# An mLSTM recurrence in one kernel: values projected with tokens on the partitions, decays of four heads joined, the loop turned by one chunk

## The chip, the cores and the metric

The kernel runs on one core of one Trainium2 chip. The metric is the device time of one execution in microseconds (us). Before the change the median of 3 runs is 1986.46 us (1985.74 to 1988.04).

## The reference, cut to what matters

One layer of a decoder: a half-step SwiGLU, a mixer, a second SwiGLU and a gated embedding, all in float32 on 1024 tokens of width 1024. The change lies in the mixer's mLSTM group (4 heads; queries and keys of 64, values of 128 numbers each):

```python
z = u @ w_in[i]
m_qk, m_v, m_o, m_if, f_q, f_k, f_v, f_f = jnp.split(z, split_idx, axis=-1)
m_qk = jax.nn.silu(causal_depthwise_conv(m_qk, conv_qk[i]))
...
# mlstm_chunkwise, per chunk: what was carried in (C), what the chunk's own tokens add (P)
D = jnp.where(causal, b[..., :, None] - b[..., None, :] + log_i[..., None, :], -jnp.inf)
P = jnp.exp(D - m_t[..., None]) * jnp.einsum("bhcld,bhcsd->bhcls", q, k)
num = (w_inter[..., None] * jnp.einsum("bhcld,bhcde->bhcle", q, C_prev)
       + jnp.einsum("bhcls,bhcse->bhcle", P, v))
C_new = decay[..., None, None] * C + jnp.einsum("bhl,bhld,bhle->bhde", w, k_c, v_c)
...
y_m = head_rmsnorm(h_m, mlstm_out_norm[i]) * jax.nn.sigmoid(m_o)
```

## The kernel before, in words

Large products are done three times in a rounded float32 (fp32r): `mm3` (L118) multiplies high by high, high by low and low by high part. A projection of 128 columns of `w_in` is a job of `proj_stream`: for each half of the tokens, 8 steps over the depth, each step 3 matmuls of 128x512, all 24 into one PSUM bank, which a "sink" then empties. The weights were split into parts earlier and lie in DRAM (`wD`); `ready_cols` loads a job's four tiles (`whi`, `wlo`, 256 KB each), one job ahead.

`mlstm` runs four stages. First the gates and the query and key columns are projected (`qk_sink`), with the gates' arithmetic woven between. Half of the gates' product was made earlier and goes through DRAM: `begun` is stored to `eD` and loaded as `G` (L791, L819). Then the values are projected: the result has value columns on the partitions, so `v_sink` copies it (`vt`) and `v_turn` transposes it, four 128x128 pieces at a time (L966), into `v1`, where tokens are on the partitions. Then the recurrence, `main`, goes through 8 chunks of 128 tokens; the projection of the output gates (`fill`, 64 steps) is woven between its pieces by estimated costs. Last, FoX attention begins with its own projections into `acc`.

A chunk of `main` has these pieces on TensorE:

- decays: `d` gets the mask (L1009, 128x512) and for each of the 4 heads one small product that spreads a row of 36 partitions (L1012, `sel` as weights); ScalarE makes `E` from it.
- scores: `st`, 4 products of 64 rows (L1023), and two transposes of the keys (L1031) for `kw`.
- outputs: for each pair of heads the carried state times the queries (L1039, 128x258) and the scores times the values (L1041, twice 128x129), into `num`.
- state: for each pair `dl` (L1044, 128x258), which VectorE adds into the state `C`.

These are plain float32, and each float32 product stands in the profile as two matmul records. After chunks 3 and 7 `back` transposes the normalised rows `ysb` (L1088), multiplies by the output gate and stores them. A scheduler of the framework moves instructions of neighbouring pieces past each other within limits, so the built order differs a little from the written one.

Of the kernel before, what the change touches and what calls it, by code (L numbers as in the profile page):

```python
# [9 lines left out]
F32 = mybir.dt.float32  # L10
# [6 lines left out]
P = 128  # L17
# [666 lines left out]
def proj_stream(N, xt, jobs, bank=None, begun=None):  # L684
# [5 lines left out]
    nxt = begun or get(0)  # L690
# [38 lines left out]
def run_all(gen):  # L729
    for _ in gen:  # L730
        pass
# [9 lines left out]
class Mix:  # L741
# [14 lines left out]
    def consts(self, pool):  # L756
# [9 lines left out]
        nc.vector.tensor_copy(out=self.mask_r, in_=m)  # L766

# [36 lines left out]
    def gates(self, xt, keep, gp, bank):  # L804
# [101 lines left out]
        s32 = t("X", shape=(36, 6, P))  # L906
        nc.gpsimd.memset(s32, 0.0)
        for row in (0, 32):
            nc.gpsimd.affine_select(out=s32[row:row + 4, 0:4, :], in_=s32[row:row + 4, 0:4, :], pattern=[[-1, 4], [0, P]],
                                    compare_op=ALU.not_equal, fill=1.0, base=0, channel_multiplier=1)  # L910
            nc.gpsimd.affine_select(out=s32[row:row + 4, 4:6, :].rearrange("p a (b c) -> p a b c", b=2),
                                    in_=s32[row:row + 4, 4:6, :].rearrange("p a (b c) -> p a b c", b=2),
                                    pattern=[[-2, 2], [-1, 2], [0, 64]],
                                    compare_op=ALU.not_equal, fill=1.0, base=0, channel_multiplier=1)
        self.sel = keep.tile([36, 6, P], F32R, tag="sel", name="sel")
# [3 lines left out]
    def mlstm(self, xt, keep):  # L919
        nc, N = self.nc, self.N  # L920
        with ExitStack() as ctx:
            pool = lambda name, **kw: ctx.enter_context(self.tc.tile_pool(reuse_waits="tile", name=name, **kw))
            mk, mps = pool("mk", bufs=1), pool("mps", bufs=1, space=PSUM)
            mt = None
            qk = mk.tile([P, 4, S], F32, tag="qk", name="qk")
            v1 = mk.tile([P, NCH, 4, 129], F32, tag="v1", name="v1")
            G1 = mk.tile([P, 4, S], F32, tag="G1", name="G1")
            qw = mk.tile([P, 2, S], F32, tag="qw", name="qw")
            dec = mk.tile([P, 2, NCH], F32, tag="dec", name="dec")
            nc.gpsimd.memset(v1[:, :, :, 128:129], 1.0)  # L930
            zin = {}

            def qk_sink(ct):
                def sink(half, acc):
# [4 lines left out]
                    zh = zt[:, 3 + half * 512:515 + half * 512]  # L939
                    if acc is None:  # L940
# [14 lines left out]
            def v_sink(hd):  # L955
                def sink(half, acc):
                    vt = mt.tile([P, 512], F32, tag="vt", name="vt")
                    nc.scalar.copy(out=vt, in_=acc)
                    turned.append((vt, half, hd))
                return sink  # L960

            def v_turn():
                vt, half, hd = turned.pop(0)
                pt = N.tr()
                for j in range(4):
                    nc.tensor.transpose(pt[:, j, :], vt[:, j * P:(j + 1) * P], N.ident)  # L966
                nc.vector.tensor_copy(out=v1[:, 4 * half:4 * half + 4, hd, 0:128], in_=pt)

# [8 lines left out]
            bank = lambda: mps.tile([P, 512], F32, tag="num", name="pj", bufs=2)  # L977
# [5 lines left out]
            turned = []  # L983
# [3 lines left out]
            v_turn()  # L987

            def main():

                for pr in range(2):
                    wb = mk.tile([P, S], F32, tag="zin", name="wb", bufs=2)
                    for half in range(2):
                        d = mps.tile([P, 512], F32, tag="D", name="wd")
                        nc.tensor.matmul(d, self.sel[:, 4 + pr, :], self.RW[:, half * 512:half * 512 + 512],
                                         start=True, stop=True)
                        nc.scalar.activation(out=wb[:, half * 512:half * 512 + 512], in_=d, func=AF.Exp)
                        yield 0.22
# [3 lines left out]
                C = [mk.tile([P, 258], F32, tag=f"C{pr}", name=f"C{pr}") for pr in range(2)]  # L1002
                for pr in range(2):
                    nc.gpsimd.memset(C[pr], 0.0)
                ysb, todo = {}, []
                for c in range(NCH):
                    ts = slice(c * P, c * P + P)
                    d = mps.tile([P, 4, P], F32, tag="D", name="d")
                    nc.tensor.matmul(d.rearrange("p a b -> p (a b)"), self.mask_r, self.ident_r.unsqueeze(1).to_broadcast([P, 4, P]),  # L1009
                                     start=True, stop=False)  # L1010
                    for hd in range(4):
                        nc.tensor.matmul(d[:, hd, :], self.sel[:, hd, :], self.R[:, ts], start=False, stop=hd == 3)  # L1012
                    E = mt.tile([P, 4, P], F32, tag="E", name="E")
# [3 lines left out]
                    yield 0.9  # L1017
                    PT = mt.tile([P, 2, 2, P], F32, tag="PT", name="PT")
                    for a in range(2):
                        o = 64 * a  # L1020
                        st = mps.tile([P, 2, P], F32, tag="ST", name="st", bufs=2)
                        for pr in range(2):
                            nc.tensor.matmul(st[:, pr, :], qk[o:o + 64, 2 + pr, ts], qk[o:o + 64, pr, ts], start=True, stop=True)  # L1023
                        nc.vector.scalar_tensor_tensor(out=PT[:, :, a, :], in0=st, scalar=0.125, in1=E[:, a:4:2, :],
                                                       op0=ALU.mult, op1=ALU.mult)
                    yield 0.9

                    if c < NCH - 1:
# [3 lines left out]
                        kw = mt.tile([P, 4, 64], F32, tag="kw", name="kw", bufs=1)  # L1032
                        nc.vector.tensor_tensor(out=kw, in0=kt[:, 0:2, :].rearrange("p a (b c) -> p (a b) c", b=2),
                                                in1=self.tok[:, c, 1, :].unsqueeze(2).to_broadcast([P, 4, 64]), op=ALU.mult)
                        yield 0.3
                    for pr in range(2):
# [5 lines left out]
                        if c < NCH - 1:  # L1042
                            dl = mps.tile([P, 258], F32, tag="D", name="dl")
                            nc.tensor.matmul(dl, kw[:, 2 * pr:2 * pr + 2, :].rearrange("p a c -> p (a c)"),  # L1044
                                             v1[:, c, 2 * pr:2 * pr + 2, :].rearrange("p a c -> p (a c)"), start=True, stop=True)
                            for a in range(2):
                                Cd = C[pr][64 * a:64 * a + 64, 129 * a:129 * a + 129]
                                dd = dl[64 * a:64 * a + 64, 129 * a:129 * a + 129]
                                if c == 0:
                                    nc.vector.tensor_copy(out=Cd, in_=dd)  # L1050
                                else:
                                    nc.vector.scalar_tensor_tensor(out=Cd, in0=Cd, scalar=dec[64 * a:64 * a + 64, pr, c:c + 1],
                                                                   in1=dd, op0=ALU.mult, op1=ALU.add)
                        yield 1.4

                        dn = N.sp.tile([P, 2], F32, tag="dn2", name="dn2")
                        nc.vector.tensor_copy(out=dn, in_=num[:, :, 128])
                        nc.vector.scalar_tensor_tensor(out=dn, in0=dn, scalar=-1.0, in1=dn, op0=ALU.mult, op1=ALU.max)
                        nc.vector.tensor_tensor(out=dn, in0=dn, in1=self.tok[:, c, 2, 2 * pr:2 * pr + 2], op=ALU.max)
                        nc.vector.scalar_tensor_tensor(out=dn, in0=dn, scalar=EPS, in1=dn, op0=ALU.mult, op1=ALU.mult)  # L1060
                        sq = mt.tile([P, 2, P], F32, tag="sq", name="sq", bufs=1)
                        nc.scalar.activation(out=sq, in_=num[:, :, 0:128], func=AF.Square)
                        ss = N.sp.tile([P, 2], F32, tag="ss2", name="ss2")
                        nc.vector.tensor_reduce(out=ss, in_=sq, axis=AX.X, op=ALU.add)
                        nc.vector.scalar_tensor_tensor(out=dn, in0=ss, scalar=1.0 / 128, in1=dn, op0=ALU.mult, op1=ALU.add)
                        r = N.rsqrt(dn)
                        if c % 4 == 0:
                            ysb[c // 4, pr] = (mk, mt)[c // 4].tile([P, 2, 4, P], F32, tag=("zin", "ysb")[c // 4], name="ysb", bufs=2)
                        nc.vector.tensor_tensor(out=ysb[c // 4, pr][:, :, c % 4, :], in0=num[:, :, 0:128],
                                                in1=r.unsqueeze(2).to_broadcast([P, 2, P]), op=ALU.mult)  # L1070
                    if c % 4 == 3:
                        todo += [(c // 4, pr) for pr in range(2)]
                    for item in [x for x in todo if x[1] in opened]:
                        todo.remove(item)
                        yield from back(ysb[item], *item)
                while todo:
                    if todo[0][1] in opened:
                        yield from back(ysb[todo[0]], *todo.pop(0))
                    else:
                        yield None  # L1080
# [553 lines left out]
```

## Time and profile before

| what | value |
|---|---|
| median of 3 runs | 1986.46 us |
| the profiled execution: its time, its span | 1986.16 us, 1984.3 us |
| TensorE (PE) busy | 1949.5 us, 98% of the span |
| VectorE (DVE), ScalarE (ACT), GpSimd (POOL) busy | 67%, 44%, 5% |
| granted TensorE clock, mean | 0.999 of full speed |

The profile shows for each engine when each instruction ran. PE is matmul, PEld weight load, SP the engine that issues DMAs. Matmuls overlap: a record of 0.39 us may be followed by the next one 0.23 us later, so what a matmul costs is read from start to start, not from its duration.

### The profile page before, as it was taken

The numbers are of one execution on the slowest core, as the hardware profiler recorded it, in microseconds if no ns is written. First come the engines' busy times: TensorE is split into PE (matmuls) and PEld (weight loads), VectorE is DVE, ScalarE is ACT, GpSimd is POOL, SyncE is SP. The second block draws the span as 40 slices with busy tenths as digits, with TensorE's granted clock in tenths as the row PEclk, the third lists the DMA queues.
The fourth block names the chain that finished last, engine by engine and source line by source line (L and its number), as shares of the span: only waits on it lengthen the run. The fifth ranks groups of instructions, "written<-read, shape, count | busy, mean of one in ns | idle before, by whom it ended". The sixth has DMA issues, their size and how long they took to land. (4 is left out here: it accounts for less than half of the span.)

```text
span 1984.3 us, 25653 instructions
## 1 busy us (share of the span) xinstructions
PE 1949.5 (98%) x9155; PEld 1607.3 (81%) x9155; DVE 1325.5 (67%) x2295; ACT 876.5 (44%) x1686; POOL 97.2 (5%) x118
## 2 busy tenths in 40 slices
PE   7999999999999999999999999999999999999998
PEld 6788888888888888778888888788888888888786
DVE  7877766776877762554665766965665565877766
ACT  6544444444445332334555543533333333445444
POOL 1100000000000110110000001200000000000011
PEclk9999999999999999999999999999999999999999
DMA  7877877778533343133222846632333337633322
GB/s 276 261 245 233 270 243 237 253 234 297 187 96 112 103 148 101 52 127 109 75 79 81 299 149 229 224 110 80 111 113 95 100 118 271 210 107 108 122 75 85
DMA packets 251920, 318.70 MB, mean 161 GB/s; under 512 B 16440, under 2 KB 158288, under 8 KB 251024
## 3 DMA queue, kind: packets, MB, share of 16 engines
q1 hardware_dynamic: 251792, 317.06, 48.5%
q8 instruction: 72, 1.18, 0.3%
q14 instruction: 56, 0.46, 0.1%
HBM read 205.73 MB, written 107.09 MB: 158 GB/s over the span
## 5 line engine op out<-in xcount | busy, mean ns | idle before, releaser
L118 PE MATMUL pp<-xhi,whi 128*128 128x512 f32 x704 | 275.1, 391 | 2.1 <-DVE xn L238 1.5
L118 PE MATMUL pp<-xhi,wlo 128*128 128x512 f32 x704 | 274.8, 390 | 0.0
L118 PE MATMUL pp<-xlo,whi 128*128 128x512 f32 x704 | 274.0, 389 | 0.0
L118 PE MATMUL dn<-xhi,whi 128*128 128x512 f32 x528 | 205.6, 389 | 0.1
L118 PE MATMUL dn<-xlo,whi 128*128 128x512 f32 x528 | 205.4, 389 | 0.0
L118 PE MATMUL dn<-xhi,wlo 128*128 128x512 f32 x528 | 205.1, 389 | 0.0
L125 ACT CAST whi<-raw 128x512 fp32r<-128x512 f32 x152 | 94.0, 622 | 172.8 <-PE pp L118 118.9
L125 ACT CAST whi<-ar 128x512 fp32r<-128x512 f32 x132 | 82.3, 623 | 195.5 <-PE dn L118 180.4
L118 PEld LDWEIGHTS pp<-xhi,whi 128*128 128x128 f32 x704 | 132.1, 188 | 30.7 <-DVE xn L238 1.3
L118 PEld LDWEIGHTS pp<-xlo,whi 128*128 128x128 f32 x704 | 132.7, 188 | 27.9 <-DVE xlo L126 0.3
L118 PEld LDWEIGHTS pp<-xhi,wlo 128*128 128x128 f32 x704 | 132.2, 188 | 27.8
L126 DVE TENSOR_TENSOR wlo<-ar,whi 128x512 fp32r<-128x512 f32 x132 | 90.8, 688 | 77.9 <-ACT whi L125 77.7
L126 DVE TENSOR_TENSOR wlo<-raw,whi 128x512 fp32r<-128x512 f32 x152 | 103.8, 685 | 43.2 <-ACT whi L125 27.4
L118 PEld LDWEIGHTS dn<-xhi,whi 128*128 128x128 f32 x528 | 99.1, 188 | 21.0 <-DVE t L311 0.5
L118 PEld LDWEIGHTS dn<-xlo,whi 128*128 128x128 f32 x528 | 99.1, 188 | 20.7
L118 PEld LDWEIGHTS dn<-xhi,wlo 128*128 128x128 f32 x528 | 99.1, 188 | 20.5
L125 ACT CAST vhi<-S 128x512 fp32r<-128x512 f32 x88 | 54.7, 621 | 104.7 <-PE pp L118 73.0
L125 ACT CAST whi<-S 128x512 fp32r<-128x512 f32 x88 | 54.6, 620 | 98.4 <-PE pp L118 52.8
L130 POOL TENSOR_TENSOR r<-v,mhalf 128x1 f32<-128x1 f32 (+1 forms) x56 | 43.7, 781 | 1094.8 <-DVE v L139 725.6
L126 DVE TENSOR_TENSOR wlo<-S,whi 128x512 fp32r<-128x512 f32 x88 | 62.0, 704 | 51.8 <-ACT whi L125 37.6
L118 PE MATMUL pj<-xhi,whi 128*128 128x512 f32 x200 | 84.6, 423 | 0.9 <-ACT zin L943 0.8
L126 DVE TENSOR_TENSOR tl<-tr,th 128x512 fp32r<-128x512 f32 (+2 forms) x112 | 55.4, 497 | 42.3 <-ACT th L125 40.4
(341 smaller groups left out, 4546.2 us busy)
## 6 DMA issues: line engine op xcount, KB each, us to landing
ar<-hidD SPq DMA_DIRECT2D x60, 512.0 KB, 3.4
hidD<-t SPq DMA_DIRECT2D x110, 256.0 KB, 3.2
raw<-in_ffn_w_gate_dram SPq DMA_DIRECT2D x46, 512.0 KB, 3.9
raw<-in_ffn_w_up_dram SPq DMA_DIRECT2D x46, 512.0 KB, 4.9
wD<-whi SPq DMA_DIRECT2D x64, 256.0 KB, 2.2
wD<-wlo SPq DMA_DIRECT2D x64, 256.0 KB, 2.3
raw<-in_w_in_dram SPq DMA_DIRECT2D x24, 512.0 KB, 4.4
whi<-wD SPq DMA_DIRECT2D x48, 256.0 KB, 2.7
```

The source lines that it names most:

```text
L118: mm = lambda *a, **kw: self.nc.tensor.matmul(*a, skip_group_check=more, **kw)
L125: self.nc.scalar.copy(out=hi, in_=src)
L126: return self.nc.vector.tensor_tensor(out=lo, in0=src, in1=hi.bitcast(F32), op=ALU.subtract)
L130: self.nc.gpsimd.tensor_tensor(out=r, in0=v, in1=self.mhalf[:, :v.shape[-1]], op=ALU.pow)
```

## The change

The values are projected the other way round: the tokens' tile `xt` is the stationary operand and the weights stream past it, so tokens come out on the partitions and `v_turn` is gone. All value weights must then be there at once: two tiles `wv` of 2 MB each, filled by 8 loads of 512 KB, two at each of the first four calls of `qk_sink`. The four spreading products of a chunk become one 128x512 product of a matrix of ones with `Rb`, the rows of `R` times a 0/1 pattern `own`, made by VectorE. The loop is written out: a chunk's outputs and state and the next chunk's scores stand together, its decays come two chunks ahead, and `pump(n)` places n steps of the output gate projection (3 matmuls each). Norms of the two pairs are joined, and `num` is copied to `ysb` first.

```diff
-            for n, _ in enumerate(proj_stream(N, xt, [(C_MV + hd * P, v_sink(hd), None) for hd in range(4)], bank)):
-                if n % KT == 3 and turned:
-                    v_turn()
+            loads = [(i, part) for i in range(4) for part in range(2)]
+            def load_wv():
+                for i, part in loads[:2]:
+                    nc.sync.dma_start(out=wv[part][:, i].bitcast(F32), in_=N.wD[:, 4 + i, part, :].rearrange("p (k n) -> p k n", k=KT))
+                del loads[:2]
...
+            for c in range(NCH):
+                acc = bank()
+                ts = slice(c % 4 * P, c % 4 * P + P)
+                for k in range(KT):
+                    xh, xl = xt[c // 4][k // 4]
+                    N.mm3(acc, xh[:, k % 4, ts], xl[:, k % 4, ts], wv[0][:, :, k, :], wv[1][:, :, k, :], k == 0, k == KT - 1)
+                nc.scalar.copy(out=v1[:, c, :, 0:128], in_=acc.rearrange("p (a b) -> p a b", a=4))
...
-                    for hd in range(4):
-                        nc.tensor.matmul(d[:, hd, :], self.sel[:, hd, :], self.R[:, ts], start=False, stop=hd == 3)
+                    nc.vector.tensor_tensor(out=rb[0:36], in0=self.R[:, chunk(c)].bitcast(F32).unsqueeze(1).to_broadcast([36, 4, P]),
+                                            in1=self.own.unsqueeze(2).to_broadcast([36, 4, P]), op=ALU.mult)
+                    nc.tensor.matmul(flat, self.ones_r, rb.rearrange("p a b -> p (a b)"), start=False, stop=True)
...
+                for c in range(NCH):
+                    nums = outputs(c)
+                    state(c)
+                    if c + 1 < NCH:
+                        scores(c + 1)
+                    norm(c, nums)
...
+                    pump(2 if c == 0 else 4)
+                    if c + 2 < NCH:
+                        decays(c + 2)
+                    pump(2 if c == 0 else 4)
```

What the built programs do with it is shown at three places. First PE where the values are projected. Before, the rows are fill after fill, and each bank's transposes follow after a few steps of the next one (`vt` is the copied bank):

```order
L118 MATMUL pj<-xhi,whi 128x512
L118 MATMUL pj<-xlo,whi 128x512
L118 MATMUL pj<-xhi,wlo 128x512
L966 MATMUL tr<-ident,vt 128x128 x4
L118 MATMUL pj<-xhi,whi 128x512
```

After the change, with buffer numbers (`wv_6277` is the high, `wv_6281` the low part; the first row is the last of the key projection):

```order
L118 MATMUL pj_6580<-xhi_5784,wlo_6492 128x512
L118 MATMUL pj_6664<-wv_6277,xhi_5778 128x512
L118 MATMUL pj_6664<-wv_6281,xhi_5778 128x512
L118 MATMUL pj_6664<-wv_6277,xlo_5779 128x512
L118 MATMUL pj_6664<-wv_6277,xhi_5778 128x512
```

Nothing but such rows stands there now, 192 of them, where 192 projections and 32 transposes stood.

Second, PE in a chunk of the loop. Before, the decays, one step of `fill`, and the scores:

```order
L1009 MATMUL d<-ident_r,mask_r 128x512
L1012 MATMUL d<-R,sel 128x128 x4
L118 MATMUL pj<-xhi,whi 128x512
L118 MATMUL pj<-xlo,whi 128x512
L118 MATMUL pj<-xhi,wlo 128x512
L1023 MATMUL st<-qk 128x128 x4
L118 MATMUL pj<-xhi,whi 128x512
```

After, the decays stand between two runs of 12 projections:

```order
L118 MATMUL pj<-xlo,whi 128x512
L118 MATMUL pj<-xhi,wlo 128x512
L1024 MATMUL d<-ident_r,mask_r 128x512
L1025 MATMUL d<-Rb,ones_r 128x512
L118 MATMUL pj<-xhi,whi 128x512
```

and all the rest of the chunk in one block (here with the transposes of the first `back`):

```order
L1060 MATMUL num<-C_6876,qw 128x258
L1062 MATMUL num<-v_6662,PT 128x129 x2
L1060 MATMUL num<-C_6877,qw 128x258
L1062 MATMUL num<-v_6662,PT 128x129 x2
L1073 MATMUL dl<-v_6662,kw 128x258 x2
L1037 MATMUL st<-qk 128x128 x4
L1041 MATMUL tr<-ident,qk 128x128 x2
L1142 MATMUL tr<-ident,ysb 128x128 x4
```

The four float32 pieces that `fill` used to part are now next to each other, and 24 projections follow instead of 21. From the first FoX projections that follow the last `ysb` transposes, PE's order is the same in both programs.

Third, SP's queue while the gates are projected. Before:

```order
L791 DMA eD<-begun 128x512
L813 DMA gbias<-in_b_fox_f_dram 8x1
L819 DMA G<-eD 128x512
L1380 DMA hr<-hD 128x1024
L791 DMA eD<-begun 128x512
L1380 DMA hr<-hD 128x1024
L89 DMA whi<-wD 128x512
```

After, with five of the eight loads of `wv` ahead of `G` (one more stands above this piece):

```order
L941 DMA wv<-wD 128x1024 x2
L795 DMA eD<-begun 128x512
L941 DMA wv<-wD 128x1024 x2
L823 DMA G<-eD 128x512
L795 DMA eD<-begun 128x512
L941 DMA wv<-wD 128x1024
L89 DMA whi<-wD 128x512
L953 DMA zin<-eD 128x512
L89 DMA wlo<-wD 128x512
```

The loads of `wv` have moved in front of the store to `eD` and the load of `G`; the loads of `hr`, which belong to a later stage, come after them.

## Rows read from the trace of the kernel before

**Rows 1.** Two stretches: busy us (records) by engine; clock, DMA share, GB/s.

```profile
699.00:710.00 11.00, 11.00 (x52) 9.03 (x51) 0.96 (x2) 6.31 (x8) 0.00 (x0) 1.00 0.81 272
...
815.00:825.00 10.00, 10.00 (x55) 7.71 (x53) 5.54 (x23) 2.38 (x7) 1.39 (x2) 1.00 0.16 53
```

**Rows 2.** Waits of PE from 745 to 889 us.

```profile
PE num L1041 <- DVE PT L1024: 0.4, 1, 0.4
PE d L1009 <- DVE C L1052: 0.4, 1, 0.4
```

**Rows 3.** Timeline of PE, a run of projections: start, duration, instruction.

```profile
730.02 0.39 PE L118 MATMUL pj<-xhi,whi 128*128 128x512 f32 x1
...
737.50 0.39 PE L118 MATMUL pj<-xhi,whi 128*128 128x512 f32 x1
```

**Rows 4.** Timeline of PE, the transposes of one value bank.

```profile
777.10 0.60 PE L966 MATMUL tr<-ident,vt 128*128 128x128 f32 x4
...
778.48 0.39 PE L118 MATMUL pj<-xlo,whi 128*128 128x512 f32 x1
```

**Rows 5.** Timeline of PE, one chunk of the loop.

```profile
815.09 0.47 PE L1009 MATMUL d<-ident_r,mask_r 128*128 128x512 f32 x1
815.49 0.66 PE L1012 MATMUL d<-R,sel 36*128 36x128 f32 x4
...
816.64 0.40 PE L118 MATMUL pj<-xhi,wlo 128*128 128x512 f32 x1
...
817.62 0.33 PE L1031 MATMUL tr<-ident,qk 128*128 128x128 f32 x1
817.86 0.50 PE L118 MATMUL pj<-xhi,whi 128*128 128x512 f32 x1
818.19 0.40 PE L118 MATMUL pj<-xlo,whi 128*128 128x512 f32 x1
...
819.46 0.60 PE L1039 MATMUL num<-C,qw 128*128 128x258 f32 x2
...
820.34 0.60 PE L1044 MATMUL dl<-v,kw 128*128 128x258 f32 x2
...
821.01 0.39 PE L118 MATMUL pj<-xlo,whi 128*128 128x512 f32 x1
...
824.96 0.46 PE L1009 MATMUL d<-ident_r,mask_r 128*128 128x512 f32 x1
```

**Rows 6.** Timeline of PE, a 128-column mask product in the FoX stage.

```profile
921.92 0.22 PE L1202 MATMUL acc<-mask_r,ident_r 128*128 128x128 f32 x1
921.98 0.45 PE L1203 MATMUL acc<-k,q 68*128 68x512 f32 x1
```

**Rows 7.** Groups of ACT, 793 to 892 us: busy us, mean ns, idle before.

```profile
L1015 ACT ACTIVATE E<-d,tok 128x128 f32<-128x128 f32 x32 | 9.1, 368 | 12.7 <-PE d L1012 12.7
...
L997 ACT ACTIVATE wb<-wd 128x512 f32<-128x512 f32 x4 | 2.4, 598 | 2.5 <-PE wd L995 2.5
L997 ACT ACT_TABLE_LOAD x1 | 1.3, 1283 | 0.0
```

**Rows 8.** Groups of DVE from 793 to 892 us.

```profile
L1024 DVE SCALAR_TENSOR_TENSOR PT<-st,E 128x256 f32<-128x256 f32 x16 | 6.1, 419 | 7.6 <-PE st L1023 5.0 <-ACT E L1015 2.6
...
L126 DVE TENSOR_TENSOR ylo<-yg,yhi 128x512 fp32r<-128x512 f32 x8 | 5.5, 688 | 1.6 <-DMA yD<-ylo 0.7 <-ACT yhi L125 0.7
```

**Rows 9.** Timeline of SP's issues while the gates are projected.

```profile
694.15 0.35 SPq L791 DMA_DIRECT2D eD<-begun  x1
...
696.21 0.35 SPq L819 DMA_DIRECT2D G<-eD  x1
```

**Rows 10.** ACT there; in brackets its idle time and what ended it.

```profile
699.48 0.72 ACT L820 ACTIVATE G<-G,gbias 128x512 f32<-128x512 f32 x1 [0.93 <-DMA G<-eD]
...
705.29 0.69 ACT L820 ACTIVATE G<-pj,gbias 128x512 f32<-128x512 f32 x1 [4.14 <-PE pj L118]
```

**Rows 11.** Timeline of PE, later in the gates' stage.

```profile
722.40 0.50 PE L118 MATMUL pj<-xhi,whi 128*128 128x512 f32 x1 [0.83 <-ACT zin L943]
```

More of the change, by code (lines that the diff above doesn't have):

```diff
@@ L681, in weave, with proj_stream @@
         assert cost is not None
-def proj_stream(N, xt, jobs, bank=None, begun=None):
+def proj_stream(N, xt, jobs, bank=None, begun=None, first=None):
     def get(j):
@@ L953, in qk_sink @@
                 return sink
[L955 to L967, printed above, removed]
             def o_sink(hd):
@@ L1016, in main, with scores @@
                                              bias=self.tok[:, c, 0, hd:hd + 1])
[L1017 to L1026, printed above, removed]
+                def scores(c):
+                    ts = chunk(c)
+                    sts = [mps.tile([P, 512], F32, tag="ST", name="st", bufs=2)[:, 0:256].rearrange("p (a b) -> p a b", a=2) for _ in range(2)]
+                    for pr in range(2):
+                        for a in range(2):
+                            o = slice(64 * a, 64 * a + 64)
+                            nc.tensor.matmul(sts[a][:, pr, :], qk[o, 2 + pr, ts], qk[o, pr, ts], start=True, stop=True)
                     if c < NCH - 1:
@@ L1041, in main @@
                             nc.tensor.matmul(num[:, a, :], PT[:, pr, a, :], v1[:, c, 2 * pr + a, :], start=c == 0, stop=c == 0 or a == 1)
[L1042 to L1066, printed above, removed]
+                        nums.append(num)
@@ new lines, in outputs, with state @@
+                    return nums
+                def state(c):
+                    if c == NCH - 1:
+                        return
+                    kw = kws.pop(c)
+                    dls = []
+                    for pr in range(2):
+                        dl = mps.tile([P, 258], F32, tag="D", name="dl") if pr else N.tr("dl").rearrange("p a b -> p (a b)")[:, 0:258]
+                        nc.tensor.matmul(dl, kw[:, 2 * pr:2 * pr + 2, :].rearrange("p a c -> p (a c)"),
+                                         v1[:, c, 2 * pr:2 * pr + 2, :].rearrange("p a c -> p (a c)"), start=True, stop=True)
+                        dls.append(dl)
+                    for pr, dl in enumerate(dls):
+                        for a in range(2):
+                            Cd = C[pr][64 * a:64 * a + 64, 129 * a:129 * a + 129]
+                            dd = dl[64 * a:64 * a + 64, 129 * a:129 * a + 129]
+                            if c == 0:
+                                nc.vector.tensor_copy(out=Cd, in_=dd)
+                            else:
+                                nc.vector.scalar_tensor_tensor(out=Cd, in0=Cd, scalar=dec[64 * a:64 * a + 64, pr, c:c + 1],
+                                                               in1=dd, op0=ALU.mult, op1=ALU.add)
@@ new lines, in main @@
+                decays(0)
+                pump(0)
+                scores(0)
+                decays(1)
+                pump(2)
+                for c in range(NCH):
+                    if c == 7:
+                        self.first = N.ready_cols(TILES.index(C_FV))
+                    nums = outputs(c)
[3 more added lines that the diff above has]
+                    norm(c, nums)
+                    for item in [x for x in todo if x[1] in opened][:1]:
+                        todo.remove(item)
+                        back(ysb[item], *item)
+                    pump(2 if c == 0 else 4)
+                    if c + 2 < NCH:
+                        decays(c + 2)
+                    pump(2 if c == 0 else 4)
@@ L1071, in main @@
                     if c % 4 == 3:
                         todo += [(c // 4, pr) for pr in range(2)]
[L1073 to L1080, printed above, removed]
+                pump(64)
@@ L1082, in back @@
+                for item in todo:
+                    back(ysb[item], *item)
             def back(y, half, pr):
@@ L1093, in back, with pump @@
                     self.put_y(mt, hd, half, yg)
-                    yield 0.5
             opened = []
-            fill = proj_stream(N, xt, [(C_MO + hd * P, o_sink(hd), None) for hd in range(4)])
-            weave(main(), fill, 0.9)
+            fill = proj_stream(N, xt, [(C_MO + hd * P, o_sink(hd), None) for hd in range(4)], first=first)
+            def pump(n):
+                for _ in range(n):
+                    next(fill, None)
+            main()
     def put_y(self, pool, k, half, src, gain=None, bufs=2, tags=("yhi", "ylo")):
@@ L1341, in attention @@
                     yield tick()
-            run_all(proj_stream(N, xt, jobs(0), bank))
+            run_all(proj_stream(N, xt, jobs(0), bank, first=self.first))
             self.wf = []
```

96 lines of the change are left out of this document (68 added, 28 removed).

## The prediction

> **What bounds the kernel now.** I first read the busy times by stretch, to see which engine the mLSTM stage waits for. In the loop PE is busy 10.00 of 10 us at clock 1.00 (the 2.4 GHz level), VectorE 5.54 and ScalarE 2.38 [rows 1]. Then the waits: from 745 us, where the value projection starts, to 889 us, where the last transposes of the stage are done, PE waits twice, 0.4 us each [rows 2]. So nothing is late there. The time goes into the instructions on PE themselves and into what it costs to pass from one kind to the next, and only a change in that list can win much. Third, the timeline of PE read from start to start. In an undisturbed run 33 projections start within 737.50 - 730.02 = 7.48 us, 0.227 us each [rows 3]. Against this price I measure everything else.
>
> **The value projection.** It keeps its 192 matmuls of 128x512. Which operand is stationary and which streams is exchanged; weight loads are as many as before. What goes is the transposes. One bank: from 777.10 to 778.48 us there are four transposes and four projections; 1.38 - 4 x 0.227 = 0.47 us [rows 4]. Eight banks: **3.8 us less**. The VectorE copies behind them vanish too, but nobody waited for them.
>
> The new streaming operand lies in four pieces of 128 columns. No row before has such an operand. From below it costs nothing more. From above, a piece may cost what a separate 128-column product does, 0.06 us [rows 6], so 0.24 in place of 0.227: 192 x 0.013 = 2.5 us. I take nothing, since the pieces stay one instruction.
>
> **The decays.** Before: from 815.09 to 816.64 us stand the mask, four spreading products and two projections, 1.55 - 0.45 = 1.10 us [rows 5]. The mask's own step is 0.40 us, so the four products and the return cost 0.70. After: mask and one 128x512 product with all 128 partitions, between projections of the same kind. The new product should cost one step, 0.227; the mask between 0.227 and its present 0.40. Together 0.45 to 0.63; I take 0.50, nearer to the low end because the mask's next weights no longer have 36 rows. Saved 0.60 a chunk, eight chunks: **4.8 us less** (3.8 to 5.2). VectorE gets one product of 36x512 a chunk, priced by the 128x512 subtraction at 0.69 us [rows 8]; it has over 4 us of idle time in each 10 [rows 1].
>
> A rule of the Trainium skill speaks against this term. TensorE: Matmul & The Clock Gate, section "Back-to-back issue gap", has a matmul cost its columns at 2.4 GHz plus about 2.5 ns; four of 128 columns would then cost as much as one of 512. The 0.70 us above against 0.227 does not agree with it; by the rule alone this term would be near nothing.
>
> **The rest of the chunk.** The chunk takes 824.96 - 815.09 = 9.87 us and holds 21 projections (4.77); less the decays, 4.00 us remain [rows 5]. Its pieces: a state product and two value products 820.34 - 819.46 = 0.88, twice; `dl` up to the second projection after it 821.01 - 820.34 - 0.227 = 0.44, twice; scores from 816.64 to 817.62 less one projection, 0.75; first transpose 0.24; second about 0.11; the return to projections 818.19 - 817.86 - 0.227 = 0.10 [rows 5]. Set side by side, the block needs 1.76 + 0.88 + 0.65 (no change of kind ahead of the scores) + 0.35 + 0.10 = 3.74. Saved 0.26, eight chunks: **2.1 us less**. The two old waits of 0.4 us go as well, since 24 projections now stand behind each block: **0.8 us less**. A floor for this part is 0.8, a ceiling about 3.2 if the scores' pairs overlap better.
>
> **New waits.** In a steady chunk I see none. The longest chain is `dl`, four updates of `C` on VectorE, next outputs; between lie 24 projections, 5.4 us. `d` has one buffer and is shared with `dl`: `E` takes 4 x 0.37 = 1.5 us [rows 7], behind the decays, and 12 projections (2.7 us) hide it. If that cover were gone it would cost PE 1.5 us a chunk.
>
> At the loop's start there is less cover. One table load 1.28, four exponentials 2.4, `Rb` at most 0.69, `E` 1.5, `PT` 0.84 make a chain of 6.7 us [rows 7, 8], without the wide product for `qw` and the hand-overs. PE has 21 projections (4.8 us), two decays (1.0), scores and transposes (1.0), one `dl` (0.44) and the four products for `wd` at 0.23 or more, 8 us or so in all, and then for the first chunk only few projections. I take **1.0 us more** for start and end of the loop. Nothing is the lower bound; 3 us the upper one, two unhidden `E`.
>
> **The loads.** `wv` is 8 x 512 KB in place of 16 x 256 KB, but now all in the gates' stage. Five stand ahead of `G` in SP's queue. `eD` was stored at 694.15, `G` issued at 696.21 and used at 699.48 after ScalarE had waited 0.93 us for it [rows 9, 10]. In the busiest stretch nearby the DMA engines moved 272 GB/s at share 0.81 [rows 1]; 512 KB take 1.9 us at that speed. One load was issued long before; four can be ahead: 4 x 1.9 = 7.7 us, so `G` would be there at about 706 instead of 699.48. ScalarE's next job was only due at 705.29 [rows 10], which hides most of it. What comes late after that is the gates' chain, on which PE already waits 0.83 us at 722.40 [rows 11]; this wait grows by the delay. **0.3 us more**, bounds 0 and 3. SP's queue holds the weights of the next key columns behind `wv` as well, but these are a whole job (10.9 us) ahead. The late loads of `hr` serve a stage hundreds of us away. The values' own weights are needed at 745 us and stand in SP's queue between the weights of the first key jobs.
>
> **Sum.** 3.8 + 4.8 + 2.1 + 0.8 - 1.0 - 0.3 = 10.2 us. The profiled execution took 1986.16 us, 0.3 under the median of the runs shown. 1986.16 - 10.2 + 0.3 gives 1976.3; I say 1976.2.
>
> **Rivals.**
>
> *The dense block makes its own waits.* Where `fill` parted the pieces, VectorE had time between them. If each chunk loses 0.6 us to a hand-over (a `C` update queued behind a norm that waits for GpSimd, say), 8 x 0.6 = 4.8, and the time is 1981. For it: before, PE waited only where work was bunched [rows 2]. Against it: 5.4 us of projections per chunk and a VectorE that is half idle [rows 1]. 0.12.
>
> *A matmul costs its columns and nothing else.* Then joining four products and grouping pieces saves nothing, and only the transposes go, 8 x 4 x 0.11 = 3.5 us at the 0.11 of the second key transpose; less 1.3 of new waits, the time is about 1984. For it: the 128-column mask product of the FoX stage costs 0.06 us, a quarter of 0.227 [rows 6]. Against it: the 0.70 of four such products with 36 rows [rows 5]. 0.05. This is the rule of the skill named above.
>
> *The change doesn't do what it says: the pieces stream slower.* At 0.24 the time is 1978.7; from 0.282 a matmul on (192 x 0.055 = 10.5) it is no faster. 0.05, nearly all of it at the mild end.
>
> *Slower: the loads starve the gates' stage.* Place: `G` and the first weights of the key columns behind `wv`. If each of the three loads of key weights, at 1.9 us for every `wv` ahead, came after the matmul that needs it and `G` 7 us late, PE would stand still for up to 12 us, and the time would be 1988. It decides from 10 us of such waits on. Against it: a share of 0.81 in the busiest stretch leaves room [rows 1], and the `hr` loads no longer stand there. 0.06. The Trainium skill, DMA: Bandwidth & Descriptors, section "Queues, rings and completion order", says that an issuing engine owns one ring on each DMA engine and that descriptors are consumed in ring order; by that, `G` does queue behind `wv`. The load of `G` landing 3.3 us after its issue is too little to show it here.
>
> **How the numbers follow.** Forecast 0.72, rivals as above. The forecast's terms alone span about 1973 (all at their best, no waits: 13 us) to 1979. To 1982.2 the range takes in the dense block's waits, the slow pieces, or start and `G` at their upper bounds together. What is left out is the columns rule and the slower case, and some tails. No change is within 0.2% of the median, 4 us, about what a measurement tells. Faster takes the forecast, most of the first rival and the mild pieces: 0.87; same 0.08; slower 0.05.
>
> **What would show it.** Right: no L966 on PE and 192 value projections 0.227 us apart; mask and L1025 together about 0.5 us; from the end of the key projection to the last `ysb` transposes some 11 us less than before; PE's waits in the loop under 2 us; the wait at 722 us about as long as now. Wrong: value projections over 0.25 us apart; waits of PE on `num` or `d` in every chunk; ScalarE waiting several us for `G` and PE behind it.

## The result: 12.4 us faster, and where they came from

The changed kernel takes 1973.99 us (median of 4 runs, 1971.42 to 1975.25), the kernel before 1986.39 us (4 runs, 1985.74 to 1988.04). The ratio is 0.9936, 95% interval 0.9924 to 0.9948. The profiled execution took 1973.56 us, its span is 1971.8 us.

To find the place I use two marks that both kernels have: ScalarE's last copy of keys and queries, and TensorE's first FoX product. Here they are in the timeline of the kernel before (start, duration, instruction, and in brackets ScalarE's idle time ahead of it):

```profile
745.41 0.58 ACT L943 COPY zin<-pj 128x512 f32<-128x512 f32 x1 [4.81 <-PE pj L118]
...
881.82 0.48 PE L118 MATMUL acc<-xhi,whi 128*128 128x512 f32 x1
```

and in that of the changed kernel, with two turns of `y` that stand a little later:

```profile
745.04 0.59 ACT L955 COPY zin<-pj 128x512 f32<-128x512 f32 x1 [4.81 <-PE pj L118]
...
868.71 0.48 PE L118 MATMUL acc<-xhi,whi 128*128 128x512 f32 x1
...
875.00 0.66 PE L1142 MATMUL tr<-ident,ysb 128*128 128x128 f32 x4
875.41 0.48 PE L118 MATMUL acc<-xhi,wlo 128*128 128x512 f32 x1
```

The stage went from 136.41 to 123.67 us, 12.74 less. Four turns of `y` stand behind the mark, where two stood before. A turn takes 0.41 us and some 0.15 more beside it, so 1.1 us are only moved: the 71st FoX product starts 18.02 us behind the mark now, and 16.91 before. **11.6 to 11.7 us are saved in the stage**; the first mark comes 0.4 us earlier as well, less than it scatters in the table below, and the rest is the drift of later stages.

The second stretch of [rows 1], in the changed kernel (busy us and records of PE, weight loads, VectorE, ScalarE, GpSimd; granted clock, DMA share, GB/s):

```profile
815.00:825.00 10.00, 10.00 (x61) 8.16 (x57) 5.57 (x19) 3.31 (x9) 1.01 (x1) 1.00 0.00 0
```

PE is still busy all the time in the loop, at clock 1.00, but for one pause of 0.11 us ahead of a turn of `y` at 845.94 us, too short for the list of its waits. The list, from 670 to 895 us:

```profile
PE pj L118 <- ACT zin L955: 0.8, 1, 0.8
PE tr L168 <- DVE xlo L126: 0.4, 1, 0.4
```

Both lie ahead of the first mark. The two of [rows 2] are gone, and none has come in the loop, not even at its start. One steady chunk, to set beside [rows 5]:

```profile
811.95 0.60 PE L1060 MATMUL num<-C,qw 128*128 128x258 f32 x2
812.38 0.61 PE L1062 MATMUL num<-v,PT 128*128 128x129 f32 x4
812.83 0.60 PE L1060 MATMUL num<-C,qw 128*128 128x258 f32 x2
813.26 0.61 PE L1062 MATMUL num<-v,PT 128*128 128x129 f32 x4
813.71 1.04 PE L1073 MATMUL dl<-v,kw 128*128 128x258 f32 x4
814.67 0.71 PE L1037 MATMUL st<-qk 64*128 64x128 f32 x8
815.32 0.44 PE L1041 MATMUL tr<-ident,qk 128*128 128x128 f32 x2
815.51 0.48 PE L118 MATMUL pj<-xhi,whi 128*128 128x512 f32 x1
815.83 0.39 PE L118 MATMUL pj<-xlo,whi 128*128 128x512 f32 x1
...
818.12 0.40 PE L118 MATMUL pj<-xhi,wlo 128*128 128x512 f32 x1
818.36 0.39 PE L1024 MATMUL d<-ident_r,mask_r 128*128 128x512 f32 x1
818.58 0.39 PE L1025 MATMUL d<-Rb,ones_r 128*128 128x512 f32 x1
818.81 0.40 PE L118 MATMUL pj<-xhi,whi 128*128 128x512 f32 x1
...
821.58 0.60 PE L1060 MATMUL num<-C,qw 128*128 128x258 f32 x2
```

Read it from start to start. Mask and joined product take 818.81 - 818.36 = 0.45 us (0.50 was forecast). The chunk takes 821.58 - 811.95 = 9.63 us and holds 24 projections (5.45), so the rest of it is 9.63 - 5.45 - 0.45 = 3.73 (3.74 was forecast). `dl` and the scores are float32 products, with two records each.

The prediction named one more sign, the time from the last copy of keys and queries to the last turn of `y`, which was to shrink by some 11 us. From mark to start of the last turn it shrank by 9.8 (886.67 - 745.41 and 876.46 - 745.04), since 27 FoX products now stand ahead of that turn in place of 19; with these 8 x 0.227 = 1.8 us it is the 11.6 from above.

The value products, one of each three in the first column and 45 steps of three between the two rows:

```profile
753.00 0.39 PE L118 MATMUL pj<-wv,xlo 128*128 128x512 f32 x1
...
784.50 0.40 PE L118 MATMUL pj<-wv,xlo 128*128 128x512 f32 x1
```

31.50 us for 135 products, 0.2333 us each, against 0.227 in [rows 3]. `G`, to set beside [rows 10]:

```profile
702.22 0.72 ACT L824 ACTIVATE G<-G,gbias 128x512 f32<-128x512 f32 x1 [2.00 <-DMA G<-eD]
704.88 0.69 ACT L824 ACTIVATE G<-pj,gbias 128x512 f32<-128x512 f32 x1 [1.94 <-PE pj L118]
```

It came 2.7 us later than before, and the next job, which waits for PE, was not held up: 704.88 against 705.29.

### The profile page after: what moved, and what is told of

Read it like the earlier page. It is cut to its first block, busy times and chain, and to the rows that moved or that the text cites. A ratio compares the mean times of both kernels' runs of the same rounds, so it can differ in the third digit from the quotient of the medians.

```text
span 1971.8 us, 25453 instructions
## 1 busy us (share of the span) xinstructions
PE 1939.4 (98%) x9099; PEld 1601.4 (81%) x9099; DVE 1318.7 (67%) x2257; ACT 883.4 (45%) x1702; POOL 94.3 (5%) x112
## 5 line engine op out<-in xcount | busy, mean ns | idle before, releaser
L118 PE MATMUL acc<-xhi,whi 128*128 128x512 f32 x192 | 76.9, 400 | 0.0
```

Of the source, the lines that this page charges most:

```text
L118: mm = lambda *a, **kw: self.nc.tensor.matmul(*a, skip_group_check=more, **kw)
```

## The experiments

Each is an edit of the changed kernel. "Stage" is the time between the two marks above, "rest" the span from the second mark on; both are worked out from starts in the timelines as above. From the second mark on, the instructions of TensorE, VectorE, ScalarE and SP stand in the same order in the changed kernel and in all experiments.

| kernel | total, median (range) us | first mark | second mark | stage | rest |
|---|---|---|---|---|---|
| before | 1986.39 (1985.74-1988.04) | 745.41 | 881.82 | 136.41 | 1102.5 |
| changed | 1973.99 (1971.42-1975.25) | 745.04 | 868.71 | 123.67 | 1103.1 |
| e1 one piece | 1973.48 (1971.93-1977.35) | 745.49 | 869.17 | 123.68 | 1102.5 |
| e2 old values | 1981.27 (1980.27-1982.81) | 745.36 | 872.14 | 126.78 | 1107.5 |
| e3 old decays | 1979.90 (1978.39-1985.22) | 744.51 | 872.38 | 127.87 | 1105.2 |
| e4 four full | 1976.62 (1975.57-1979.90) | 744.99 | 870.38 | 125.39 | 1103.4 |
| e5 parted | 1976.45 (1973.17-1977.21) | 746.21 | 869.65 | 123.44 | 1104.8 |
| e6 loads first | 1975.76 (1975.04-1977.58) | 745.80 | 869.50 | 123.70 | 1103.8 |
| e7 order | 1974.08 (1971.96-1976.13) | 746.01 | 869.71 | 123.70 | 1102.6 |
| e8 mask on GpSimd | 1975.40 (1972.77-1978.17) | 744.79 | 866.96 | 122.17 | 1106.7 |
| e9 loads ahead of `G` | 1971.92 (1971.54-1974.43) | 742.85 | 866.54 | 123.69 | 1103.3 |
| e10 changed, again | 1973.41 (1972.48-1982.11) | 744.96 | 868.66 | 123.70 | 1102.7 |
| e11 e8, again | 1976.01 (1974.08-1976.70) | 746.87 | 869.04 | 122.17 | 1106.0 |

The stage repeats to 0.03 us where its code is the same or should be. The rest does not: it spreads over 5 us. So an edit here is judged by its stage.

**e1, the streaming operand in one piece.**

```diff
-[P, 4, KT, P] ... wv[part][:, i]      ... wv[0][:, :, k, :], wv[1][:, :, k, :]
+[P, KT, 4, P] ... wv[part][:, :, i, :] ... wv[0][:, k], wv[1][:, k]
```

> The eight value weight loads write the 512 columns of one contraction step as one stretch, so that the streaming operand of a product is one piece of 512 instead of four pieces of 128, and each load writes 512-byte stretches. Theory (the four pieces cost 6 ns a product): the 192 products come back from 0.2333 to 0.227 us each, start to start, and the total falls by 1.2 us against the changed kernel. Rival (the pieces are free, the 0.233 comes from elsewhere): 0.233 as in the changed kernel, total unchanged within 0.3 us. A second rival (the loads with shorter stretches land later): PE's wait for the gates near 722 us grows from 0.8 us, and the total rises by up to 2 us.

The value products in its timeline, 28 steps of three apart:

```profile
754.85 0.39 PE L118 MATMUL pj<-wv,xlo 128*128 128x512 f32 x1
...
774.45 0.39 PE L118 MATMUL pj<-wv,xlo 128*128 128x512 f32 x1
```

19.60 / 84 = 0.2333 us, and the stage is the same to 0.01 us. My theory of the pieces is refuted. PE's wait of 0.8 us in the gates' stage is unchanged too, so the shorter stretches of the loads cost it nothing.

**e7, another order of the three products.** It asks the next question about the 0.2333.

```diff
-N.mm3(acc, xh[:, k % 4, ts], xl[:, k % 4, ts], wv[0][:, :, k, :], wv[1][:, :, k, :], k == 0, k == KT - 1)
+nc.tensor.matmul(acc, xh[:, k % 4, ts], wv[0][:, :, k, :], start=k == 0, stop=False)
+nc.tensor.matmul(acc, xl[:, k % 4, ts], wv[0][:, :, k, :], start=False, stop=False)
+nc.tensor.matmul(acc, xh[:, k % 4, ts], wv[1][:, :, k, :], start=False, stop=k == KT - 1)
```

> In the value projection the three products of a step stand in the order hi-hi, lo-hi, hi-lo: the streaming operand stays the same for two products in a row and the loaded one changes every time, where in the changed kernel the loaded one stays for two. Theory (the 0.2333 us a product, of which e1 showed that the four pieces are not the reason, comes from the orientation, tokens loaded and weights streamed, whatever the order): 0.233 again, time unchanged within 0.3 us. Rival (it is the loaded operand that repeats): a product comes to 0.227, 1.2 us faster.

The stage takes 123.70 us, as before the edit. Neither pieces nor order are the reason. Nor is the orientation by itself, which this run leaves over: the FoX output projection loads tokens and streams weights too, and its code and order are the same in both programs; 15 of its products take 3.40 us in the kernel before (1196.50 to 1199.90 us, 0.227 each) and 3.50 in the changed one (1184.42 to 1187.92 us, 0.2333 each).

**e2, the values projected as before the change.**

```diff
-for c in range(NCH): ... N.mm3(acc, xh, xl, wv[0], wv[1], ...)
+for n, _ in enumerate(proj_stream(N, xt, [(C_MV + hd * P, v_sink(hd), None) ...], bank)):
+    if n % KT == 3 and turned: v_turn()
```

> The values are projected as before the change (weights streaming past tokens, then sixteen times four transposes in the way back to tokens on the partitions); decays and the grouped chunk stay as in the changed kernel. Theory (my sum, with the 0.233 us a product that the changed kernel shows): 2.5 us slower than the changed kernel. Rival (the term of 3.8 us was right, and the loads in the gates' stage had cost something elsewhere): 3.8 us slower or more in the value stage and faster before it. Rival (the whole gain is in the values): 12 us slower.

The stage is 3.1 us longer. One turn in its timeline:

```profile
777.03 0.60 PE L989 MATMUL tr<-ident,vt 128*128 128x128 f32 x4
777.38 0.49 PE L118 MATMUL pj<-xhi,whi 128*128 128x512 f32 x1
777.71 0.39 PE L118 MATMUL pj<-xlo,whi 128*128 128x512 f32 x1
```

777.71 - 777.03 - 0.227 = 0.45 us a turn, 3.6 in all, less 192 x 0.0063 = 1.2 for the slower products of the new form: 2.4 us. Read directly, the first key transposes, which stand behind the last turn, start 796.24 - 745.36 = 50.88 us behind the first mark, and 793.31 - 745.04 = 48.27 in the changed kernel, 2.6 less. Of the 0.5 us that come after it, 0.25 are a new wait for `Rb`, and the rest arises where the built order differs at the start of the loop. So the value term is near the theory's 2.5 and under the rival's 3.8, though the stage as a whole lies between the two; the 12 of the other rival is out. The total is 7.3 us longer, because the rest is 4.4 us longer. The largest part of that stands in the waits and the busy times of the FoX stage there, 1028 to 1048 us:

```profile
PE acc L1259 <- DMA k<-k: 1.0, 1, 1.0
```

```profile
1028.00:1038.00 10.00, 8.38 (x58) 7.20 (x57) 6.62 (x13) 6.17 (x15) 0.00 (x0) 1.00 0.55 153
1038.00:1048.00 10.00, 10.00 (x56) 9.20 (x56) 7.61 (x21) 6.58 (x23) 1.64 (x1) 0.83 0.00 1
```

PE stood waiting for a copy of `k`, was busy 8.38 of 10 us, and in the next 10 us was granted 0.83 of the clock: up to 1041.6 us it ran some 3.4 us at the lower of its two levels (1.2 GHz). In the changed kernel the clock is 1.00 there, and this wait is not in its list. Between 1025 and 1041 us this execution fell 2.7 us further behind the changed kernel, 1.3 up to the end of the wait and 1.4 at the lower clock. Why the copy comes later, I did not find. This kernel also tells about the loads, since it has no `wv`: its stretch from the first copy of `begun` (693.37) to the first mark is 51.99 us, 52.00 with the loads (from 693.04).

**e3, the four spreading products in the new place; e4, the joined product cut into four.**

```diff
-nc.tensor.matmul(flat, self.ones_r, rb.rearrange("p a b -> p (a b)"), start=False, stop=True)
+for hd in range(4):   # e3
+    nc.tensor.matmul(d[:, hd, :], spread[:, hd, :], self.R[:, chunk(c)], start=False, stop=hd == 3)
+for hd in range(4):   # e4
+    nc.tensor.matmul(d[:, hd, :], self.ones_r, rb[:, hd, :], start=False, stop=hd == 3)
```

> In place of the one product of 512 columns that joins the decays, the four products of 128 columns with 36 weight rows stand in the same place, eight times; the vector operation that prepares the joined operand is gone with it. Theory (these four cost 0.85 us together and the joined one 0.23): 0.62 us a chunk, 5 us slower in all. Rival (a product costs its columns, four of 128 are as dear as one of 512): 0 to 0.5 us slower.

> The joined product is cut into four of 128 columns each with the same 128-row weights and the same joined operand. Theory (what was dear in the four old products was their 36 weight rows, and the change from 128 rows to 36 and back): four at about 0.06 us each, total 0 to 0.5 us slower. Rival (what was dear is that there were four of them, each with a start of its own): 0.6 us a chunk, 4 to 5 us slower, as with the four old ones.

Timeline of PE in e3, mask to second projection:

```profile
830.08 0.40 PE L1021 MATMUL d<-ident_r,mask_r 128*128 128x512 f32 x1
830.41 0.66 PE L1023 MATMUL d<-R,s 36*128 36x128 f32 x4
831.00 0.50 PE L118 MATMUL pj<-xhi,whi 128*128 128x512 f32 x1
831.34 0.40 PE L118 MATMUL pj<-xlo,whi 128*128 128x512 f32 x1
```

and in e4:

```profile
829.02 0.39 PE L1024 MATMUL d<-ident_r,mask_r 128*128 128x512 f32 x1
829.25 0.56 PE L1026 MATMUL d<-Rb,ones_r 128*128 128x128 f32 x4
829.65 0.44 PE L118 MATMUL pj<-xhi,whi 128*128 128x512 f32 x1
829.93 0.39 PE L118 MATMUL pj<-xlo,whi 128*128 128x512 f32 x1
```

The same stretch takes 0.69 us in the changed kernel, 0.91 in e4 and 1.26 in e3. Both of my alternatives for e4 were too simple. Cutting 512 columns into four products costs 0.22 us a chunk (1.72 in the stage); weights of 36 rows cost 0.35 more, spread over the product ahead of them (0.33 in place of 0.23), themselves, and the return (0.34). Together 4.2 us of stage, against the 4.8 of the prediction's term.

The weight loads (PEld) of e3 show where the 36 rows pay:

```profile
829.85 0.19 PEld L1021 LDWEIGHTS d<-ident_r,mask_r 128*128 128x128 f32 x1
830.41 0.52 PEld L1023 LDWEIGHTS d<-R,s 36*128 36x128 f32 x4 [0.37 <-issue]
```

The mask's weights are loaded from 829.85 us, 0.23 ahead of their product, while the product before it still runs. The load of the first 36-row product starts at 830.41, together with that product. So it is at every change between 128 rows and 36 or 64 in the loops of e3 and of the changed kernel: the load starts within 0.03 us of its own product, where one between two projections starts some 0.22 us ahead. The load is not hidden at such a change; why not, no run shows.

**e5, the block parted.**

```diff
+one = 1 if 0 < c else 0
 nums = outputs(c)
+pump(one)
 state(c)
+pump(one)
 if c + 1 < NCH: scores(c + 1)
+pump(one)
 norm(c, nums)
...
-pump(2 if c == 0 else 4)
+pump(2 if c == 0 else 1)
```

> From the second chunk on, one projection step of the o gate (three products) stands again behind the outputs, one behind the state products and one behind the scores, so that the dense block is parted in three; the number of steps in a chunk stays eight. Theory of the prediction (each departure from the projections and each return to them costs PE about 0.1 us, which is why the grouped block saves): two more departures and two more returns, 0.3 us a chunk, 2 to 2.5 us slower than the changed kernel. Rival (only a change between weights of 128 rows and of fewer costs; the changed kernel's rows show 0.217 us for a product with C right behind a projection, which is no surcharge): the only new such place just moves the surcharge of 0.09 us from the last product for dl to the projection ahead of the scores, so the time is unchanged within 0.3 us.

Timeline of PE, one parted block:

```profile
824.11 0.61 PE L1062 MATMUL num<-v,PT 128*128 128x129 f32 x4
824.47 0.48 PE L118 MATMUL pj<-xhi,whi 128*128 128x512 f32 x1
824.79 0.39 PE L118 MATMUL pj<-xlo,whi 128*128 128x512 f32 x1
...
825.25 1.03 PE L1073 MATMUL dl<-v,kw 128*128 128x258 f32 x4
825.93 0.58 PE L118 MATMUL pj<-xhi,whi 128*128 128x512 f32 x1
826.36 0.40 PE L118 MATMUL pj<-xlo,whi 128*128 128x512 f32 x1
826.59 0.40 PE L118 MATMUL pj<-xhi,wlo 128*128 128x512 f32 x1
826.92 0.72 PE L1037 MATMUL st<-qk 64*128 64x128 f32 x8
```

The four products for `num` and the projection behind them take 824.79 - 824.11 = 0.68 us, as 4 x 0.11 + 0.23 would: the projection starts 0.08 early and is longer by as much. `dl` with its projection takes 826.36 - 825.25 = 1.11, as four half products of 0.22 and 0.23 would. Only the projection ahead of the scores pays, 0.33, and `dl` no longer does. The stage is 0.2 us shorter, not 2 us longer: going to a projection and back is free here as long as the weights on both sides have 128 rows.

**e6 and e9, the loads.** In e6 all loads are issued with the first key job:

```diff
-for i, part in loads[:2]:
+for i, part in loads[:8]:
...
-del loads[:2]
+del loads[:8]
```

> All eight loads of the value weights are issued at once, with the first job of the gates' stage, in place of two with each job. Theory (the loads are covered with about 2.7 us to spare in the changed kernel, where ScalarE used G at 702.22 and its next job was due at 704.88): three more loads stand ahead of G, G comes at about 706 to 708, PE's wait near 722 us grows from 0.8 to 2 or 3 us, and the time rises by 1 to 2.5 us. Rival (the loads go by on other engines of the DMA and G does not see them): wait 0.8 us and time as in the changed kernel.

e6 missed its purpose: in SP's order of issues still only five loads stand ahead of `G`, and the kernel behaves as the changed one. So it decides nothing. In e9 they are issued ahead of the gates' own work, and all eight stand ahead of `G`:

```diff
-                    load_wv()
...
+            for _ in range(4):
+                load_wv()
             bank = lambda: mps.tile([P, 512], F32, tag="ST", name="pj", bufs=2)
             with self.tc.tile_pool(reuse_waits="tile", name="gp", bufs=1) as gp:
                 g = self.gates(xt, keep, gp, bank)
```

> The loads of the value weights are issued before the gates' own work, so that all eight stand ahead of G in SP's queue (five in the changed kernel), and the loads of the gates' biases behind them. Theory of the prediction (a load of 512 KB takes about 1.9 us, and G waits for those ahead of it; ScalarE's cover runs out): three more loads, G at about 707 to 708, 3 us behind the 704.88 at which ScalarE's next job was due, PE's wait near 722 us grows from 0.8 to about 3.5 us, and the time rises by 2 to 3 us. Rival (G does not wait for the whole of the loads ahead of it): G at 702 to 704, wait 0.8 us, time unchanged within 0.5 us in this stage.

ScalarE in e9:

```profile
704.39 0.69 ACT L824 ACTIVATE G<-pj,gbias 128x512 f32<-128x512 f32 x1 [5.22 <-DMA gbias<-in_b_fox_f_dram]
704.98 0.71 ACT L824 ACTIVATE G<-G,gbias 128x512 f32<-128x512 f32 x1
...
709.29 0.59 ACT L954 COPY zin<-pj 128x512 f32<-128x512 f32 x1
709.90 1.28 ACT L831 ACT_TABLE_LOAD   x1
```

With all eight loads ahead of it, `G` is there by 704.98 us, later than the rival's 704 and earlier than the theory's 707. The loads were also issued earlier, which my sum of 1.9 us for each load had left out. They do hold up what stands behind them: ScalarE waited 5.22 us for the gates' bias, whose load was issued at 700.07 us. PE did not suffer by it. Its wait of 0.8 us for `zin` is gone from PE's list, for a reason that neither theory had: the copy of `zin` now stands ahead of the last table load on ScalarE (711.32 in the changed kernel, behind both). From the first copy of `begun` (691.99) to the first mark it takes 50.86 us; in all the other kernels of the table it takes 51.96 to 52.00. This is the fastest version that I ran: 1971.92 us, ratio to the kernel before 0.9928 (0.9915 to 0.9940), beside 0.9937 (0.9924 to 0.9949) for the changed kernel in the same session. The intervals overlap; the 1.1 us are sure only in the stretch from `begun` to the first mark.

**e8 and its repetition, a product less.**

```diff
+if c < 2:
     nc.tensor.matmul(flat, self.mask_r, ...)
...
+if c > 1:
+    nc.gpsimd.affine_select(out=E, in_=E, pattern=[[0, 4], [1, P]], compare_op=ALU.is_ge, fill=0.0, ...)
```

> From the third chunk on the causal mask is no product on TensorE any more: the exponentials are taken without it, and GpSimd sets the part ahead of the diagonal to zero in E, in place, two chunks ahead of its use. Theory (PE's list of products sets the time of this stage, and a product that goes takes its 0.229 us with it): six products, 1.4 us faster than the changed kernel. Rival (GpSimd, at some 2 us for 128x512 judging by its 0.71 us for 128x128, comes late for PT, and PE waits for PT in each chunk): some tenths of a us a chunk, 1 to 3 us slower.

> The changed kernel once more, unaltered, on the chip of the two beside it. It measures how far a total of the same program moves from one job to the next and where: the median 1973 to 1976 us, and the mLSTM stage (from the last eviction of keys and queries to the last rows of y) 127.1 us within 0.1.

> The mask on GpSimd from the third chunk on, unaltered, beside the changed kernel. Theory (the 1.5 us gained in the mLSTM stage is certain, and what the end of the program took back in the first look, 3.4 us, is how its waits happened to fall): stage 125.6 us again, total 1 to 2 us under the changed kernel. Rival (the waits of the last stage follow from the time at which it is reached, so the same program loses the same): the last stage again 2 us or more longer than in the changed kernel, total equal or up to 2 us over it.

The group on GpSimd, 795 to 870 us (busy, mean ns of one, idle before):

```profile
L1032 POOL TENSOR_SCALAR_AFFINE_SELECT E<-E 128x512 f32<-128x512 f32 x6 | 3.8, 636 | 15.6 <-ACT E L1029 15.6
```

0.64 us each, nobody waits for it, and the stage is 1.50 us shorter both times, where six products at 0.229 make 1.4. This confirms that PE's list sets the time here. The stage of e10, 123.70, repeats that of the changed kernel. But the total does not fall: the rest is 3 to 4 us longer, in both executions of this program, and 1103.1 and 1102.7 in both of the changed one. The sums are alike, the places are not. From 1830 us of the changed kernel on, in the last stage, e8 is 3.4 us longer than the changed kernel and e11 only 1.1 longer than e10; e11 had lost 2.2 us before, half of it in a wait of 1.1 us for a load in the FoX output. So neither forecast of e11 holds: the total is 2.6 us over that of e10, not under it, and the last stage did not lose 2 us again. Whether this program loses 3 us by its nature or happened to twice stays open; e9, which reaches the second mark 2 us earlier, does not lose them.

## Why the prediction was right

The forecast was 1976.2 us with 10.2 us saved; 12.4 were saved in the medians, 11.6 to 11.7 in the stage. Term by term:

- **What bounds it.** PE's list of instructions, with no waits to win: right, by the waits above and by e8.
- **Transposes gone, 3.8.** The turns are worth 3.6 (e2). The step that failed is the price of the new products: nothing was taken, and they cost 0.0063 us each, 1.2 in all. The bound of 2.5 held them, but not for the reason given there, as e1 shows. Net 2.4 to 2.6.
- **Decays joined, 4.8.** Mask and joined product take 0.45 in place of 0.50; e3 puts the term at 4.2 in the new surroundings.
- **Rest of the chunk, 2.1.** The size came out, 3.73 against 3.74 us, but for other reasons than those given, so it is partly luck. The pieces read before add up to 3.84 us, not to the 4.00 of the subtraction. Of the 0.16 left over, 0.10 lie in the projection ahead of the next mask, which took 0.33 us there (824.96 less the row below) and takes 0.24 now (818.36 - 818.12); ahead of other masks of the kernel before it took from 0.23 us on, so eight times 0.26 is an estimate. e5 shows that standing together saves nothing by itself. The two key transposes, now side by side, save 0.16: 815.51 - 815.32 = 0.19 us in place of 0.35. The scores' 0.10 only moved to `dl`, which takes 0.96 in place of 0.88.

```profile
824.63 0.40 PE L118 MATMUL pj<-xhi,wlo 128*128 128x512 f32 x1
```

- **Old waits, 0.8.** Gone.
- **New waits, +1.0, and `G`, +0.3.** They did not come. The cover that the prediction named (8 us of PE's work at the start of the loop, ScalarE's idle time ahead of 705 us) was enough in both places; the cautious 1.3 us were the error. `G` came at 702.2, not 706.
- By chunk the saving is 9.87 + 3 x 0.227 - 9.63 = 0.92 us (0.86 forecast), 7.4 us in eight. With 2.4 for the values and 0.8 for the waits this makes 10.6. Some 0.8 to 1 us more lies in the first and last chunks and the `wd` products; I did not divide it further.

Of the rivals, the dense block made no waits. The pieces do not stream slower (e1). The loads cost PE nothing (e2, e9). The rule that a product costs its columns is refuted by e4, where the same columns in four products cost 0.22 us more. The Trainium skill, TensorE: Matmul & The Clock Gate, section "Back-to-back issue gap", from which the prediction took that rule, gives it for a product by itself and says that it counts too little for short products in a stream; the trace agrees with this, 0.11 us for one of 128 columns where the formula gives 0.056.

The Trainium skill, TensorE: Matmul & The Clock Gate, section "LDWEIGHTS (loading the stationary operand)", says that a weight load takes its columns divided by 1.2 in ns, however many rows it has, 107 ns for 128 columns. The trace agrees as far as the distance of starts goes: products of 128 or 129 columns in a row start 0.11 us apart with 128 rows (four in 812.83 - 812.38 = 0.45 us). A load's own record is longer, 191 ns in the mean for those products from 800 to 860 us, and overlaps with the next:

```profile
L1062 PEld LDWEIGHTS num<-v,PT 128*128 128x128 f32 x48 | 7.2, 191 | 0.7
```

That the weight load is what sets the distance of 0.11 us is only argued; no run here shows it. The surcharge for 36 rows is not in that rule; e3 shows it together with a load that starts late.

## What to carry to other kernels

Where one engine is busy all the time, price the change from start to start on that engine, each product with its neighbours, and book a wait only where the cover really runs out. Short products are dear: one of 128 columns takes 0.11 us and one of 512 takes 0.23, and weights with fewer than 128 rows cost another 0.1 us ahead of them and on the way back, where their load starts only with their product. Joining or padding them to one full product pays; merely standing together did not where all weights had 128 rows (e5). Judge an edit by the length of its stage, which repeats to some hundredths of a us, since later stages give and take more than the edit is worth.

## What the runs showed that I had not expected

- Products that load tokens and stream weights start 0.2333 us apart in the value projection throughout, in one piece or four and in either order; the projections of [rows 3] take 0.227. In the FoX output the same products take 0.227 in one program and 0.2333 in the other, so neither pieces nor order nor orientation decides it. The cause is open.
- Between two projections the weights are loaded one product ahead; at a change to 36 or 64 rows and back the load starts only with its product, and some 0.1 us is lost each time (e3).
- With the same order of instructions from the first FoX product on, the rest of the program took between 1102.5 and 1107.5 us in different kernels, and differed by 0.4 and 0.8 us between two executions of the same one.
- A single wait of 1.0 us in the FoX stage, behind two smaller ones that the changed kernel has too, was followed by 3.4 us at the lower clock of 1.2 GHz (e2), which cost another 1.4 us.
